# A modulation vector moved to GpSimd, and modulation rows fetched a unit earlier, in a two-layer FoX / GLA trunk

## The chip, the cores and the metric

The kernel runs on one core of a Trainium2 chip. The metric is the device time of one execution in microseconds. The engines are TensorE (PE, with its weight loads PEld), VectorE (DVE), ScalarE (ACT), GpSimd (POOL) and SyncE (SP), which here issues the transfers. Each engine takes its instructions strictly in the order in which they stand in its queue.

## The reference

The trunk has two layers. Layer 0 mixes tokens with forgetting attention (16 heads of 64, 1024 tokens), layer 1 with gated linear attention; each is followed by a SwiGLU channel mixer with 2816 hidden columns. All is fp32.

```python
c_act = jax.nn.silu(c)
for i in range(DEPTH):                       # 2
    mod = c_act @ ada_w[i] + ada_b[i]        # 1024 -> 6 x 1024
    sh1, sc1, g1, sh2, sc2, g2 = jnp.split(mod, 6, axis=-1)
    h = modulate(rms_norm(x, norm1_g[i]), sh1, sc1)
    y = forgetting_attention(h, ...) if i == 0 else gated_linear_attention(h, ...)
    x = x + g1[:, None, :] * y
    h = modulate(rms_norm(x, norm2_g[i]), sh2, sc2)
    x = x + g2[:, None, :] * swiglu(h, ffn_w_in[i], ffn_w_out[i])
return rms_norm(x, final_g)
```

Twelve modulation vectors of 1024 values are needed, numbered here as the kernel does: j = 0 to 5 for layer 0 (sh1, sc1, g1, sh2, sc2, g2) and 6 to 11 for layer 1. Each is a product of one vector with a 1024 x 1024 matrix.

## The kernel before

**Matmuls.** Every fp32 operand is split into a high and a low part (`split`, L175 on ScalarE and L176 on VectorE), and every product is three matmuls (`mm3`, L317 to L319). The channel mixer runs a recursive 2x2 scheme with seven products in place of eight; its sums of weight blocks are made by GpSimd (L951 to L963), its sums of results by VectorE out of the accumulators (L1717), and the derived hidden blocks by GpSimd (L1677 to L1703) and split at L1595 and L1596.

**Modulation vectors.** Vectors 0 and 1 are made at the start, partly on TensorE. The others are made beside the matmuls on VectorE or GpSimd: a row block of `ada_w` is fetched (`ada_load`, L454: four transfers, each to 32 partitions), and then 128x256 blocks of it are multiplied by a column of the activated conditioning vector (`c42`) and added to an accumulator. `ada_steps` does this on VectorE, one fused multiply-add per block (L515 for the first, L517): eight loads with four blocks each where `nt` is 4, or sixteen with two where it is 2. `ada_pool` does it on GpSimd with a multiplication (L478) and an addition (L480) per block, in one buffer that is fetched again after its second block. `ada_end` (L460) closes a vector with two small matmuls with a matrix of ones in quadrants, and VectorE adds the bias (L463).

**Pacing.** These functions are generators, and a `Pace` object advances one of them: each call adds to a balance, and each `yield` takes its value from it. `ada0` holds vectors 2 and 3 (VectorE, in attention), `ada0p` vector 4 (GpSimd, in attention), and `ada1` vectors 5, 6, 7 (in the first channel mixer), 8, 9, 10 (in the second token mixer) and 11 (in the second channel mixer). In the first channel mixer `prod` calls `ada1(0.64 * n)` for each product (n is 4, or 3 or 4 in the second half), and a step takes ADA_A = 4 units between its load and its two blocks and ADA_B = 2 after them. All three vectors are finished (`ada1.flush`) before the last two groups of the first half; vector 5 is the gate of this same mixer.

**Attention.** A unit is a head and a quarter of the queries; there are eight for each pair of heads. `weave` runs the units of pair p against the q and k projections (`qk_proj`) and the v projection (`v_half`) for the next pair. A unit's score matmuls are reduced by VectorE (L1331), exponentiated by ScalarE (L1335), scaled by GpSimd (L1337), transposed by TensorE (L1357), split, and multiplied with v (L1369, L1371); VectorE and ScalarE empty the result (L1386, L1387). The projections' accumulators, two PSUM banks, are emptied in `q_evac` (L867 to L871) and `k_evac`. From the third pair on, each projection ends with `ada0(1.6)`: one or two loads, each followed at once by its four VectorE steps. The raw rows come from a ring of three buffers, `wr`, which the weight loads (`load_w`, L228, split at L243 and L247) use too.

**The order.** The kernel's text gives each instruction a place in the trace order. A planner that simulates the engines then sets the order in each engine's queue: it takes the earliest traced instruction that it holds to be ready, so an instruction may be drawn ahead of others. Where the kernel writes `tc.issue_after`, `in_order`, `behind_one` or a lag in `weave`, the order on that engine is fixed by hand. A step of `ada_steps` with `ahead` is tied behind the VectorE instruction that was traced just before it; those in attention (`ahead` is 0) are not, but for the first, which is tied behind an early instruction.

Of the kernel before, what the change touches and what calls it, by code (L numbers as in the profile page):

```python
# [53 lines left out]
def trunk(ctx, tc, x, c, ada_w, ada_b, norm1_g, norm2_g, ffn_w_in, ffn_w_out,  # L54
# [123 lines left out]
    wr = Ring(big, names[0:3])  # L178
# [75 lines left out]
    split_after = {}  # L254
# [232 lines left out]
    def ada_steps(l, j, acc, raw_of, nt, ahead):  # L487


        steps, got = deque(range(32 // nt)), deque()  # L490

        def load():
            if not steps:
                return
            n = steps.popleft()
            raw = raw_of([P, nt * 256], F32, f"ada{l}{j}{n}").rearrange("p (t c) -> p t c", t=nt)
            ada_load(raw, l, j, n, nt)
            got.append(raw)

        for _ in range(ahead):  # L500
            load()
        for n in range(32 // nt):
            load()
            if ahead:
                yield ADA_A
            raw = got.popleft()
            with ExitStack() as es:
                if ahead:
                    es.enter_context(tc.issue_after(last_of("D")))
                elif n == 0:  # L510
                    es.enter_context(tc.issue_after(split_after["D"]))
                for t in range(nt):
                    o = (0 if nt == 4 else 32) + t * (32 // nt) + n
                    if n == t == 0:
                        nc.vector.tensor_scalar(acc, raw[:, t], c42[:, o:o + 1], None, op0=ALU.mult)  # L515
                    else:
                        nc.vector.scalar_tensor_tensor(acc, raw[:, t], c42[:, o:o + 1], acc,  # L517
                                                       op0=ALU.mult, op1=ALU.add)
            yield ADA_B if ahead else 1.0
        ada_end(l, j, acc)  # L520
        yield 1.0

# [19 lines left out]
            while self.q:  # L542
                self(1.0)

    ada0, ada0p, ada1 = Pace(), Pace(), Pace()

    def ada1_queue(js, acc, raws_):
        r = Cycle(raws_)
        for j in js:
            ada1.q.append(ada_steps(*divmod(j, 6), acc, r, 2, len(raws_) - 1))  # L550
# [736 lines left out]
    def qk_proj(p, i):  # L1287

        if i == 0:
            qkt[p] = qk_tiles(p)  # L1290
        wt = feed.next()
        feed.depth = 3
        for hf in range(2):
            ps = pj([P, HALF], F32, f"qk{i}{p}{hf}")
            yield from proj(ps, wt, hT, hf)
            (k_evac if i else q_evac)(ps, qkt[p], hf)
        if p > 1:
            ada0(1.6)

    oTs = {}  # L1300

# [99 lines left out]
    def attention(p):  # L1401
        for a in range(2):
            h = 2 * p + a
            for i, g in enumerate(ORDER):
# [10 lines left out]
                elif i == 3:  # L1415
                    load_far(h + 1)
                    load_cum(h + 2)
                if p:
                    ada0p(0.8)
                if pending[0] is not None:  # L1420
                    yield from finish(*pending[0])
# [91 lines left out]
    oh = new_h("oh")  # L1513
# [38 lines left out]
    def ffn(l, oh, xs, slots, nm, mid, norm_end, each=None, blocks=None):  # L1552
# [153 lines left out]
        def prod(w, t):  # L1706
            ps = pin([P, HALF], F32, f"p{l}")
            n = len(t)
            for k in range(n):
                mm3(ps, w.hi[:, k, :], w.lo[:, k, :], hi(t[k]), lo(t[k]), k == 0, k == n - 1)  # L1710
            tick()
            ada1(0.64 * n)
            return ps

        def add(G, key, ps, src=None):
# [154 lines left out]
        for X in gs[2:]:  # L1870
            up = lambda n: advance(n) if X is gs[-1] else None
            if X is gs[-2]:
                ada1.flush()
                nxt[0] = part(0)
                advance(4)
            nc.scalar.copy(dest(X, C11), prod(feed.next(), B11))
# [84 lines left out]
        n = 4 if each else 2  # L1961
# [68 lines left out]
    slots = ffn_slots(rest)  # L2030
# [16 lines left out]
            marks["G0"] = last_of("G")  # L2047
        return gates

    def mid(*js):  # L2050
        v = Views(slots["hid"], 2, [HALF], f"ad{js[0]}").v
        ada1_queue(js, v[0][:, 0:256], v[1:4])
        ada1.at -= 20.0

    ADA_A, ADA_B = 4.0, 2.0
    ffn(0, oh, xs, slots, "fo", lambda: mid(5, 6, 7), norm_mixer)
    h1 = hs1
    after_norm = marks.pop("G0")
    split_after.update(marks)
# [557 lines left out]
```

## Time and profile before

| | us |
|---|---|
| Three runs, median (lowest, highest) | 2351.62 (2349.36, 2352.88) |
| The profiled execution, its own time | 2348.59 |
| Its span, first to last instruction | 2346.8 |
| PE busy in the span | 2321.1 (99%) |
| DVE busy | 1786.4 (76%) |
| ACT busy | 1124.0 (48%) |
| POOL busy | 1155.3 (49%) |

A row of the profile names the line of the kernel, the engine, the operation, the tile that it writes and those that it reads, the count, the busy time and the mean duration in ns, then the idle time of the engine just before these instructions and what ended it. `DMA x<-y` as a releaser is the landing of a transfer. Names end in `_s` for SBUF slots and `_b` for PSUM banks: `ad_s` and `acc_s` are modulation accumulators and rows, `ada_s` a row in attention, `mp_b` the bank in which a vector is closed, `o_s` and `xv_s` weights of the mixer, `p_b` its accumulators. In a list of waits, each row gives the engine and tile that waited, on what, and then the total, the count and the longest.

### The profile page before, as it was taken

The page shows a single profiled execution, that of the slowest core. Times are in us where ns is not written, and L with a number is a line of the kernel's source. Part 1 is how long each engine was busy: PE and PEld are TensorE (multiplying, and loading weights), DVE is VectorE, ACT ScalarE, POOL GpSimd, SP SyncE. Part 2 cuts the span into 40 slices and gives each one's busy share as a digit, 9 for nine tenths or more (in the row PEclk, how much of TensorE's full clock was granted, in tenths as well). Part 3 has the DMA queues.
Part 4 walks back from the last instruction along what each step waited for, and adds up shares of the span by engine and source line. Part 5 has one row for each costly group of instructions (what it writes and reads, how often), then busy time and mean ns, then how long its engine had stood idle before and what let it go on. Part 6 is the DMA issues. An engine that isn't in the chain of part 4 may idle for free.

```text
span 2346.8 us, 35574 instructions
## 1 busy us (share of the span) xinstructions
PE 2321.1 (99%) x12088; PEld 1977.9 (84%) x12088; DVE 1786.4 (76%) x2946; ACT 1124.0 (48%) x2166; POOL 1155.3 (49%) x1027
## 2 busy tenths in 40 slices
PE   8999999999999999999999999999999999999999
PEld 7998888888888788788888899898888888888888
DVE  6577777787788998986788666667787777876787
ACT  6566656675543333344325654345444333345236
POOL 1334545543445656564553522345456666664651
PEclk8999999999999999999999999999999999999999
DMA  8533433342425555558774443554434544458774
GB/s 265 159 91 108 120 115 109 112 153 96 153 97 174 188 181 174 163 188 315 252 269 156 135 126 101 152 171 168 149 105 159 178 144 162 139 189 302 236 263 141
DMA packets 359343, 390.72 MB, mean 166 GB/s; under 512 B 26909, under 2 KB 296377, under 8 KB 359161
## 3 DMA queue, kind: packets, MB, share of 16 engines
q1 hardware_dynamic: 359160, 388.45, 50.7%
q8 instruction: 95, 1.56, 0.3%
q14 instruction: 88, 0.71, 0.1%
HBM read 287.10 MB, written 101.25 MB: 165 GB/s over the span
## 4 chain that ended last, share of the span: by engine, by line
PE 53%; DVE 5%; issue 4%; POOL 3%; DMA 2%; ACT 1%; SPq 0%; DVEq 0%; POOLq 0%; ACTq 0%
PE p_b L317 11%; PE p_b L319 11%; PE p_b L318 11%; PE gv_b L319 1%; PE gv_b L317 1%; PE gv_b L318 1%; PE gr_b L317 1%; PE gr_b L319 1%; PE gr_b L318 1%; DVE ad_s L517 1%; DVE o_s L176 1%; PE gqp_b L317 1%; PE gqp_b L319 1%; PE gk_b L317 1%; PE gqp_b L318 1%
## 5 line engine op out<-in xcount | busy, mean ns | idle before, releaser
L175 ACT CAST o_s<-xv_s 128x512 fp32r<-128x512 f32 (+1 forms) x392 | 236.4, 610 | 326.8 <-PE p_b L319 236.7
L176 DVE TENSOR_TENSOR o_s<-xv_s,o_s 128x512 fp32r<-128x512 f32 (+1 forms) x392 | 339.9, 871 | 46.9 <-ACT o_s L175 46.3
L317 PE MATMUL p_b<-B,o_s 128*128 128x512 f32 x608 | 236.1, 391 | 2.7 <-DVE x L1717 1.8
L319 PE MATMUL p_b<-B,o_s 128*128 128x512 f32 x608 | 236.0, 389 | 0.0
L318 PE MATMUL p_b<-B,o_s 128*128 128x512 f32 x608 | 236.0, 389 | 0.0
L951 POOL TENSOR_TENSOR ex_s<-xv_s,xv_s 128x512 f32<-128x512 f32 (+1 forms) x64 | 94.8, 1481 | 251.1 <-DMA xv_s<-in_ffn_w_in_dram 128.0
L1337 POOL TENSOR_SCALAR lp_s<-lp_s,st 128x128 f32<-128x128 f32 (+7 forms) x128 | 97.3, 764 | 224.0 <-DVE st L1336 193.5
L318 PE MATMUL p_b<-T,o_s 128*128 128x512 f32 x480 | 186.7, 389 | 0.0
L317 PE MATMUL p_b<-T,o_s 128*128 128x512 f32 x480 | 186.7, 389 | 0.0
L319 PE MATMUL p_b<-T,o_s 128*128 128x512 f32 x480 | 181.3, 389 | 0.0
L317 PEld LDWEIGHTS p_b<-B,o_s 128*128 128x128 f32 x608 | 114.1, 188 | 28.2 <-DVE x L1717 2.9
L1335 ACT ACTIVATE lp_s<-lp_s,st 128x128 f32<-128x128 f32 (+7 forms) x128 | 99.3, 776 | 76.5 <-DVE st L1331 74.8
L319 PEld LDWEIGHTS p_b<-B,o_s 128*128 128x128 f32 x608 | 114.1, 188 | 23.9
L318 PEld LDWEIGHTS p_b<-B,o_s 128*128 128x128 f32 x608 | 114.2, 188 | 23.3
L953 POOL TENSOR_TENSOR xv_s<-ex_s,xv_s 128x512 f32<-128x512 f32 (+1 forms) x64 | 94.2, 1471 | 56.8 <-DVE o_s L176 53.3
L1717 DVE TENSOR_TENSOR ex_s<-ex_s,p_b 128x512 f32<-128x512 f32 x140 | 94.0, 681 | 31.7 <-PE p_b L319 31.6
L963 POOL TENSOR_TENSOR xv_s<-xv_s,xv_s 128x512 f32<-128x512 f32 x48 | 66.3, 1381 | 97.9 <-issue 56.8
L175 ACT CAST pt_s<-t_b 128x512 fp32r<-128x512 f32 (+1 forms) x160 | 79.3, 548 | 56.8 <-PE t_b L1357 55.4
L318 PEld LDWEIGHTS p_b<-T,o_s 128*128 128x128 f32 x480 | 90.1, 188 | 18.7
L319 PEld LDWEIGHTS p_b<-T,o_s 128*128 128x128 f32 x480 | 90.1, 188 | 18.7
L317 PEld LDWEIGHTS p_b<-T,o_s 128*128 128x128 f32 x480 | 90.1, 188 | 18.6
L176 DVE TENSOR_TENSOR pt_s<-t_b,pt_s 128x512 fp32r<-128x512 f32 (+1 forms) x160 | 96.3, 631 | 11.8 <-ACT pt_s L175 11.3
(1535 smaller groups left out, 7387.8 us busy)
## 6 DMA issues: line engine op xcount, KB each, us to landing
xv_s<-in_ffn_w_in_dram SPq DMA_DIRECT2D x176, 256.0 KB, 3.3
hid_B<-x SPq DMA_DIRECT2D x66, 512.0 KB, 3.0
ad_s<-in_ada_w_dram SPq DMA_DIRECT2D x448, 64.0 KB, 2.4
hid_T<-x SPq DMA_DIRECT2D x44, 512.0 KB, 2.9
xv_s<-in_ffn_w_out_dram SPq DMA_DIRECT2D x88, 256.0 KB, 3.8
T2o<-hid_T SPq DMA_DIRECT2D x22, 512.0 KB, 6.2
T1o<-hid_T SPq DMA_DIRECT2D x22, 512.0 KB, 6.3
B11o<-hid_B SPq DMA_DIRECT2D x22, 512.0 KB, 7.6
```

Of the source, the lines that this page charges most:

```text
L175: nc.scalar.copy(hi, src)
L176: nc.vector.tensor_sub(lo, src, hi.bitcast(F32))
L317: nc.tensor.matmul(ps, ah, bh, start=start, stop=False, skip_group_check=chain)
L318: nc.tensor.matmul(ps, ah, bl, start=False, stop=False, skip_group_check=chain)
L319: nc.tensor.matmul(ps, al, bh, start=False, stop=stop, skip_group_check=chain)
L517: nc.vector.scalar_tensor_tensor(acc, raw[:, t], c42[:, o:o + 1], acc, op0=ALU.mult, op1=ALU.add)
L951: nc.gpsimd.tensor_add(s1, a21, a22)
L953: nc.gpsimd.tensor_sub(a11, s1, a11)
L963: nc.gpsimd.tensor_sub(r[A12], r[A12], r[A11])
L1335: nc.scalar.activation(lp, lp, AF.Exp, bias=mcur, scale=-1.0, accum_out=st[:, qi, 2:3])
L1337: nc.gpsimd.tensor_scalar(lp, lp, st[:, qi, 3:4], 1.0, op0=ALU.mult, op1=ALU.mult)
L1717: nc.vector.tensor_add(d, d if src is None else dest(G, src), ps)
```

## The change

In the first channel mixer, vector 5 is made by `ada_pool` on GpSimd, paced by a new `Pace` called `ada1p` with 0.075 n per product; its accumulator is the second half of the first of the modulation views, its row buffer the fourth. Vectors 6 and 7 stay on VectorE, with two row buffers in place of three (so one load ahead in place of two) and with ADA_A = 6 and ADA_B = 3. In attention, a step of `ada_steps` now yields 0.5 between its load and its four VectorE instructions, and 0.5 after them, in place of 1.0 after both; no more than two other buffers of the ring may be taken in between. The calls `ada0(1.6)` at the end of the projections go, and each unit from the second pair on calls `ada0(0.4)` ahead of the GpSimd vector's `ada0p(0.8)`.

```diff
@@ ada_steps
             load()
             if ahead:
                 yield ADA_A
+            elif split_after:
+                at = wr.n
+                yield 0.5
+                assert wr.n <= at + 2
             raw = got.popleft()
...
-            yield ADA_B if ahead else 1.0
+            yield ADA_B if ahead else 0.5
         ada_end(l, j, acc)
         yield 1.0
...
-    ada0, ada0p, ada1 = Pace(), Pace(), Pace()
+    ada0, ada0p, ada1, ada1p = Pace(), Pace(), Pace(), Pace()
@@ qk_proj
             (k_evac if i else q_evac)(ps, qkt[p], hf)
-        if p > 1:
-            ada0(1.6)
@@ attention
                 if p:
+                    if p > 0:
+                        ada0(0.4)
                     ada0p(0.8)
@@ ffn
             ada1(0.64 * n)
+            ada1p(0.075 * n)
...
             if X is gs[-2]:
                 ada1.flush()
+                ada1p.flush()
@@ around the mixers
-    def mid(*js):
+    def mid(*js, pool=None):
         v = Views(slots["hid"], 2, [HALF], f"ad{js[0]}").v
-        ada1_queue(js, v[0][:, 0:256], v[1:4])
+        if pool is not None:
+            ada1p.q.append(ada_pool(*divmod(pool, 6), v[0][:, 256:512], v[3]))
+        ada1_queue(js, v[0][:, 0:256], v[1:4 if pool is None else 3])
         ada1.at -= 20.0

-    ADA_A, ADA_B = 4.0, 2.0
-    ffn(0, oh, xs, slots, "fo", lambda: mid(5, 6, 7), norm_mixer)
+    ADA_A, ADA_B = 6.0, 3.0
+    ffn(0, oh, xs, slots, "fo", lambda: mid(6, 7, pool=5), norm_mixer)
```

## The prediction

> **What bounds the kernel now.** I read the profile page first: it gives the span and says which engine fills it.
>
> ```profile
> span 2346.8 us, 35574 instructions
> PE 2321.1 (99%) x12088; PEld 1977.9 (84%) x12088; DVE 1786.4 (76%) x2946; ACT 1124.0 (48%) x2166; POOL 1155.3 (49%) x1027
> ...
> L319 PE MATMUL p_b<-T,o_s 128*128 128x512 f32 x480 | 181.3, 389 | 0.0
> ```
>
> TensorE (PE) is busy for 2321.1 of 2346.8 us. What an edit elsewhere can win is therefore time in which PE stands still, and I looked for it with the table of busy time in the two stretches where the edits lie: attention from its second pair of heads to its seventh (160 to 515 us), and the first channel mixer while its modulation vectors are made (707 to 1030 us), with the mixer's stretch after that.
>
> ```profile
> core 0: us, PE busy (x) PEld busy (x) DVE busy (x) ACT busy (x) POOL busy (x), PEclk, DMA share, GB/s
> 160.00:515.00 355.00, 349.19 (x2261) 308.01 (x2261) 260.91 (x685) 224.25 (x478) 178.02 (x256) 1.00 0.39 119
> 707.00:1030.00 323.00, 317.53 (x1398) 260.93 (x1397) 292.45 (x372) 118.52 (x207) 196.57 (x132) 1.00 0.55 177
> 1030.00:1250.00 220.00, 220.00 (x974) 182.21 (x973) 169.97 (x215) 86.00 (x155) 126.03 (x88) 1.00 0.73 253
> ```
>
> The columns are the length, then the busy time of each engine with its instructions. PE idles 355 - 349.2 = 5.8 us in attention, 323 - 317.5 = 5.5 us in the mixer's first stretch, and not at all after 1030 us. VectorE (DVE) is the contrast: 91% busy before 1030 us (292.45 of 323), 77% after (169.97 of 220). Next, the list of waits for PE in both stretches says who ends that idle time.
>
> ```profile
> PE vps_b L317 <- DVE QB L871: 1.6, 1, 1.6
> PE o_b L1371 <- DVE oT_s L1387: 1.3, 4, 0.4
> PE qk_b L317 <- DVE QB L871: 1.3, 2, 0.7
> PE s_b L1323 <- DVE st L1331: 0.8, 3, 0.3
> ...
> PE mp_b L460 <- DVE ad_s L517: 2.8, 2, 1.6
> PE p_b L317 <- DVE x L1717: 1.8, 2, 1.1
> PE p_b L317 <- DVE sg_s L1717: 0.9, 2, 0.7
> ```
>
> The first four rows are attention: about 5 us, all on DVE results. The last three are the mixer: 2.8 us on the closing matmul of a modulation vector (mp_b, L460), which needs the last DVE step of that vector, and 2.7 us on accumulators that DVE has not yet emptied (L1717). So **the ceiling of the whole change is about 11.3 us**, 0.5% of the time: PE cannot be given back more than it idles, but for the overlap of matmuls that comes below.
>
> **The change, part by part: the mixer.** One vector of three leaves DVE for GpSimd (POOL). On DVE a vector is 32 steps of 128x256; on POOL it is 32 multiplications and 31 additions, the form that attention already runs for another vector.
>
> ```profile
> 707.00:1030.00 323.00, 65.86 (x93) 1.00 0.55 177
> L517 DVE SCALAR_TENSOR_TENSOR ad_s<-ad_s,c,ad_s x130: 467/485/1520, 717.2 to 2039.0; 128x256 f32<-128x256 f32 x130
> L480 POOL TENSOR_TENSOR acc_s<-acc_s 128x256 f32<-128x256 f32 x31 | 23.2, 748 | 1.0
> L478 POOL TENSOR_SCALAR acc_s<-acc_s,c 128x256 f32<-128x256 f32 x32 | 17.0, 531 | 12.4 <-DMA acc_s<-in_ada_w_dram 12.4
> L176 DVE TENSOR_TENSOR pt_s<-t_b,pt_s 128x512 fp32r<-128x512 f32 x68 | 44.8, 685 | 5.2 <-ACT pt_s L175 5.0
> L176 DVE TENSOR_TENSOR o_s<-xv_s,o_s 128x512 fp32r<-128x512 f32 x101 | 98.7, 978 | 9.6 <-ACT o_s L175 9.5
> L1596 DVE TENSOR_TENSOR x<-x,x 128x512 fp32r<-128x512 f32 x20 | 26.2, 1316 | 3.3 <-ACT x L1595 2.5
> L1596 DVE TENSOR_TENSOR x<-sg_s,x 128x512 fp32r<-128x512 f32 x20 | 23.5, 1177 | 4.2 <-ACT x L1595 3.6
> ```
>
> Removed from DVE: 65.86 / 93 = 0.708 us a step, times 32 = **22.7 us**. Added to POOL: 32 x 0.531 + 31 x 0.748 = **40.2 us**, spread at 0.3 of a step per product. A product is 12 matmuls, so 34 steps take 113 products; at 317.5 us of PE for 1398 matmuls that is 0.227 us each, 2.73 us a product, some 310 us in all. POOL goes from 196.6 to about 237 us in 323, 61% to 73%.
>
> That POOL time is not free for DVE. The steps of L517 have a median of 0.485 us and reach 1.52; L176 takes 0.685 us in attention, where one input is an accumulator, and 0.978 us here, where both inputs lie in SBUF; L1596, also with both inputs in SBUF, takes 1.316 and 1.177. Over the plain durations (0.485, and 0.685 for the wide ones) the excess is 65.86 - 93 x 0.485 = 20.8, 101 x 0.293 = 29.6, and 20 x 0.631 + 20 x 0.492 = 22.5 us: 72.9 us of DVE waiting beside 196.6 us of POOL work, 0.37 us for each. 40.2 us more of POOL cost DVE 0.37 x 40.2 = **14.9 us**. The net relief is 22.7 - 14.9 = 7.8 us: DVE's idle time rises from 30.6 to 38.4 us, a quarter. This is much less than one vector of three suggests.
>
> The Trainium skill's page SBUF — State Buffer (Who interferes with whom) says that a DVE instruction with two SBUF inputs and a GpSimd instruction that reads SBUF exclude each other, the later one standing still until the other is done. The rows above agree in kind: only the forms with both inputs in SBUF grow.
>
> For PE: there are two DVE vectors left instead of three, so a third of the 2.8 us on mp_b goes with the count (0.9). The remaining two are paced at 6 + 3 units a step instead of 4 + 2, with 2.56 units per product, and a vector's closing matmul is traced 3 units behind its last step instead of 2; I take half of the remaining 1.9 as gone (0.95). POOL's own closing matmul is traced four products, some 11 us, behind its last addition. Of the 2.7 us behind L1717 I take a third, a little above the quarter by which DVE's idle time grows, because pairs of steps also come 3.5 products apart instead of 2.3 (0.9). With the overlap of successive matmuls that each idle gap also destroys (a 0.389 us matmul, the last row of the page above, issues every 0.227, so some 0.16 us a stop, two stops), **3.0 us**. Bounds: 5.5 us, all the idle time; and a loss, priced among the rivals, if POOL's work blocks DVE more than the mean does.
>
> ```profile
> L454 SPq DMA_DIRECT2D ad_s<-in_ada_w_dram x448: 560/587/1945, 675.1 to 2003.3; - x150
> ...
> SPq L454 <- DVE ad_s L517: 30.6, 19, 3.6
> SPq L454 <- POOL acc_s L480: 28.2, 10, 5.6
> ...
> POOL acc_s L478 <- DMA acc_s<-in_ada_w_dram: 12.4, 4, 4.4
> ```
>
> Its transfers stay on SP's queue, 64 for a vector before and after (448 for seven); what changes is whom SP waits for. In the mixer SP waits 30.6 us for DVE to leave a modulation buffer; with one buffer on POOL it waits for POOL, as in attention (28.2 us in 10 waits, 5.6 at most), with weight loads (L933) and spills (L1648) queued behind. PE has no wait for a weight tile in the rows above, and weights are fetched five ahead, five times 2.73 us; a wait of 5.6 us fits, so I cost it at nothing; without that cover it would be 5.6 us each time. POOL may also stand for its own row as in attention, 12.4 us in four waits. Delayed next would be L951 to L963, which feed those weights.
>
> **The change, part by part: attention.** The 16 loads and 64 steps of two vectors stay. They move from the ends of the q and k projections into the units: a load in one, its four steps in a later one, 0.8 of a half per unit.
>
> ```profile
> 172.22 0.69 DVE L871 SCALAR_TENSOR_TENSOR QB<-qk_b,QB 64x512 fp32r<-64x512 f32 x1
> ...
> 199.87 1.01 DVE L517 SCALAR_TENSOR_TENSOR acc_s<-ada_s,c,acc_s 128x256 f32<-128x256 f32 x2 [5.28 <-DMA ada_s<-in_ada_w_dram]
> DVE acc_s L517 <- DMA ada_s<-in_ada_w_dram: 17.7, 7, 5.4
> L517 DVE SCALAR_TENSOR_TENSOR acc_s<-ada_s,c,acc_s 128x256 f32<-128x256 f32 x55 | 33.1, 602 | 18.3 <-DMA ada_s<-in_ada_w_dram 17.7
> ...
> 130.00:160.00 30.00, 4.42 (x7) 1.00 0.34 97
> 408.00:467.00 59.00, 4.49 (x8) 1.00 0.34 108
> 467.00:515.00 48.00, 0.00 (x0) 1.00 0.51 159
> 467.00:515.00 48.00, 46.15 (x273) 38.86 (x272) 38.20 (x101) 34.30 (x70) 19.05 (x26) 1.00 0.51 159
> ```
>
> DVE stood 5.28 us at 199.87 for a row whose load had just been issued, 17.7 us in seven such waits. If every one went, DVE would have that much more room, but PE has it only where a result was late for PE: the short waits on oT_s and st, 2.1 us, and the two on QB, 2.9. I take two thirds of the short ones (1.4) and half of those on QB (1.45), 2.85 us, because two batches of four no longer follow each other at the end of a projection, just where QB is due.
>
> Against that stands the new end. Fifty-six units call the pacer with 0.4, and 18 units of work need 45 calls, that is until the second or third unit of the seventh pair. Before, no step runs after 467 us (the row of zero). Now four to eight steps of 0.602 us do, 2.4 to 4.8 us of DVE, where PE already idles 48 - 46.15 = 1.85 us. The DVE has 9.8 us free there, so most is covered; I put 0.35 us for it, with 4.8 us as the bound if none is covered. **Net 2.5 us**, between a gain of 5.8 us and a loss of 4.8. The rows' loads now stand ahead of the loads of the masks and sums on SP; what would be late next is L1331, which reads them. The weight loads share the ring of three buffers with the rows; a row held a unit longer delays the third load after it, which a projection needs only units later.
>
> **The sum.** 3.0 + 2.5 = 5.5 us. The profiled execution took 2348.59 us, 1.8 beyond its span; it becomes 2343.1. The three runs have their median 3.0 us higher, at 2351.62, so the same step gives **2346.1 us**. A measurement of this kernel tells about 0.2%, 4.7 us, from no change; my forecast lies just beyond that.
>
> **The rivals.**
>
> *The change does not do what it says* (2350.6 us). An order made by a planner need not follow the trace order. The steps at 139 us (the row 130 to 160 us holds seven) are traced behind a q projection whose accumulator DVE empties (L871) at 172 us, so steps are drawn forward until their load seems landed; a load traced a unit ahead may be drawn forward with them, and DVE would still wait. For it: POOL's rows, traced ahead already, still cost POOL 12.4 us. Then attention gives nothing, and the mixer's count alone 0.9: about 1 us.
>
> *POOL shuts DVE out* (2357.6 us, the slower side). A multiplication and an addition run back to back, 1.28 us in which no two-input DVE step proceeds. If the added POOL time costs DVE all of itself, 40.2 - 22.7 = 17.5 us are added to DVE, its idle time falls from 30.6 to 13.1 us, and the 5.5 us of PE idle time grow in proportion of the lost room, by 30.6 / 13.1, to 12.8: 7.3 us more, less 1.3 from attention. It decides from the point where a POOL us costs DVE more than 22.7 / 40.2 = 0.56 us; the rows show 0.37. The rule of the Trainium skill named above (SBUF — State Buffer, Who interferes with whom), taken at its word, gives this case when POOL always starts first; the trace agrees that DVE can stand for a whole POOL instruction (1.52 us at most on L517), though not that it always does.
>
> *Both stages lose nearly all their idle time* (2340.6 us): 11 us, if every stop is the tail of a DVE queue that was only just late. For it: none is longer than 1.6 us. Against: attention's stops recur where no step of L517 is near.
>
> **How the numbers follow.** Forecast 0.50, no effect 0.28, POOL shutting DVE out 0.12, all the idle time 0.10. Of the forecast's own 0.50, a gain of 3 to 8 us, about 0.40 lie beyond 4.7 us; with the last rival, faster has 0.50. The first rival (less 0.02) and the rest of the forecast make 0.36 for no change, and 0.14 is left for slower. The range 2340 to 2354 us reaches from all the idle time to the loss of 4.8 us in attention beside the mixer's gain (2353.4), and leaves out the slow rival and little else.
>
> **What would show it.** In the changed profile: L478 and L480 with 64 and 62 instructions, and 32 fewer on L515 and L517; DVE's share between 707 and 1030 us down by about 8 us only, and two-input durations of L176 and L1596 longer; the wait of mp_b on DVE below 1 us; no wait of L517 for a row longer than 2 us in attention; PE idle at 3 us in each stretch instead of 5.5 and 5.8. Wrong: waits of L517 for ada_s that still sum to more than 10 us; PE waiting for QB or st after 467 us for more than 3 us; any PE wait for a weight tile or for POOL in the mixer.

## The result and the profile after

The changed kernel takes 2361.31 us (median of six runs, 2359.28 to 2362.58), against 2351.19 for the kernel before in the same comparison. The ratio is 1.0043, with a 95% interval of 1.0030 to 1.0056: **slower by about 10 us**, where 5.5 us faster was forecast. The range, 2340 to 2354 us, does not hold it.

The profiled execution took 2361.16 us. From the page of the changed kernel:

```profile
span 2359.4 us, 35610 instructions
PE 2324.2 (99%) x12088; PEld 1975.5 (84%) x12088; DVE 1769.6 (75%) x2914; ACT 1123.0 (48%) x2166; POOL 1207.6 (51%) x1090
```

The table of its busy time in three of the stretches of the prediction (columns as there):

```profile
160.00:515.00 355.00, 349.11 (x2259) 307.98 (x2258) 258.53 (x679) 224.66 (x480) 179.26 (x258) 1.00 0.40 117
707.00:1030.00 323.00, 311.42 (x1347) 252.85 (x1346) 268.59 (x329) 113.53 (x199) 237.21 (x188) 0.99 0.53 171
1030.00:1250.00 220.00, 220.00 (x974) 182.27 (x973) 168.33 (x214) 85.56 (x153) 126.61 (x88) 1.00 0.72 254
```

The count of matmuls in a stretch of fixed length says how far the kernel has come. In attention it is 2259 against 2261: nothing lost, nothing won. Between 707 and 1030 us it is 1347 against 1398. The 51 missing matmuls, at the 0.227 us of the prediction, are 11.6 us of the 12.6 by which the span grew. After 1030 us PE has no idle time, as before. **Nearly the whole loss lies in the first channel mixer, while the vectors are made.**

PE idles 323 - 311.4 = 11.6 us there instead of 5.5, so 6.1 us of the 11.6 lost are more idle time (that the two sums have the same value is chance). Of the other 5.5 us, some 3 lie behind the longest stop, which ends at 869.5 us. The granted clock of PE fell to half there (stretch, length, PE busy with its instructions, granted clock, DMA share, GB/s):

```profile
865.60:869.50 3.90, 0.16 (x1) 0.92 0.77 261
869.50:875.70 6.20, 6.18 (x17) 0.50 0.40 113
```

At a clock of 0.50, 6.2 us do the work of 3.1. The kernel before has no such stretch between 707 and 1030 us, and the prediction has no term for one. The remaining 2.4 us were not traced further.

The waits of PE between 707 and 1030 us (total, count, longest):

```profile
PE p_b L317 <- DVE x L1722: 6.9, 4, 3.8
PE p_b L317 <- DVE sg_s L1722: 3.8, 4, 1.3
PE p_b L317 <- DVE ex_s L1722: 0.3, 1, 0.3
```

L1722 is L1717 of before. The wait on the closing matmul (2.8 us) is gone, as forecast, but the waits for accumulators that VectorE has not yet emptied grew from 2.7 to 11.0 us. The longest wait of GpSimd in the same stretch, with the number of its line unchanged:

```profile
POOL ad_s L478 <- DMA ad_s<-in_ada_w_dram: 21.9, 5, 6.0
```

Here GpSimd stands for its own row. And VectorE in attention, where L521 is L517 of before:

```profile
DVE acc_s L521 <- DMA ada_s<-in_ada_w_dram: 22.6, 7, 5.3
```

It still stands 22.6 us for rows, against 17.7 before, where this was to end.

### The profile page after: what moved, and what is told of

Same layout as the page of the kernel before. It is cut to its first block, busy times and chain, and to the rows that moved or that the text cites. A ratio compares the mean times of both kernels' runs of the same rounds, so it can differ in the third digit from the quotient of the medians.

```text
span 2359.4 us, 35610 instructions
## 1 busy us (share of the span) xinstructions
PE 2324.2 (99%) x12088; PEld 1975.5 (84%) x12088; DVE 1769.6 (75%) x2914; ACT 1123.0 (48%) x2166; POOL 1207.6 (51%) x1090
## 4 chain that ended last, share of the span: by engine, by line
PE 59%; POOL 5%; DVE 5%; DMA 4%; issue 3%; SPq 1%; ACT 1%; DVEq 0%; POOLq 0%; ACTq 0%
PE p_b L317 12%; PE p_b L319 12%; PE p_b L318 12%; DMA ad_s<-in_ada_w_dram 2%; PE gv_b L317 1%; PE gv_b L319 1%; PE gv_b L318 1%; PE gr_b L317 1%; PE gr_b L319 1%; PE gr_b L318 1%; DVE ad_s L521 1%; SPq L454 1%; DVE x L1600 1%; POOL sg_s L1707 1%; DVE o_s L176 1%
## 5 line engine op out<-in xcount | busy, mean ns | idle before, releaser
L176 DVE TENSOR_TENSOR o_s<-xv_s,o_s 128x512 fp32r<-128x512 f32 (+1 forms) x392 | 341.8, 877 | 47.1 <-ACT o_s L175 43.6
L1722 DVE TENSOR_TENSOR ex_s<-ex_s,p_b 128x512 f32<-128x512 f32 x140 | 93.9, 680 | 30.8 <-PE p_b L319 30.6
L247 POOL TENSOR_TENSOR w_l_s<-w__s,w_h_s 128x256 fp32r<-128x256 f32 x90 | 70.5, 812 | 68.1 <-ACT w_h_s L243 68.1
```

Source lines behind the costliest of these rows:

```text
L176: nc.vector.tensor_sub(lo, src, hi.bitcast(F32))
L247: (nc.gpsimd if i < 3 else nc.vector).tensor_sub(lo[:, cs], rw[:, cs], hi[:, cs].bitcast(F32))
L1722: nc.vector.tensor_add(d, d if src is None else dest(G, src), ps)
```

## The experiments

Medians are in us; the kernel before took between 2349.1 and 2350.3 beside them. The ratio is to it.

### Which half of the change

`attention_only` has the mixer of before; `mixer_only` has the attention of before.

```diff
# attention_only
-    ADA_A, ADA_B = 6.0, 3.0
-    ffn(..., lambda: mid(6, 7, pool=5), norm_mixer)
+    ADA_A, ADA_B = 4.0, 2.0
+    ffn(..., lambda: mid(5, 6, 7), norm_mixer)
# mixer_only: ada0(1.6) again at the ends of the projections, no ada0(0.4) in the units, 1.0 after a step
```

> The attention part alone; the first mixer makes vectors 5, 6, 7 on VectorE with 4 + 2 units as before. If the loss lies in the mixer, the time is that of before within 3 us (2348 to 2354), and TensorE idles about 5 us in attention as in both profiles. If the loss lies in attention, it is 2358 or more. The prediction's own price for this part is 2.5 us of gain.

> The mixer part alone; attention as before. If the loss lies in the mixer: 2359 to 2364, with VectorE waiting some 25 to 30 us for ScalarE's casts of the hidden blocks (7 us before) and TensorE idling about 11 us between 707 and 1030 us. If it lies in attention, or only both together make it: within 3 us of before. The prediction's price for this part is 3.0 us of gain.

Measured: attention_only 2349.21, ratio 0.9998 (0.9989 to 1.0007); mixer_only 2360.1, ratio 1.0043 (1.0030 to 1.0056). The attention half does nothing that can be measured, and the mixer half is the whole loss. In attention_only VectorE's wait for rows is there as well:

```profile
DVE acc_s L521 <- DMA ada_s<-in_ada_w_dram: 22.4, 7, 5.3
```

Seven waits, 5.3 us the longest, as before the change. Tracing the load a unit earlier did not part it from its steps: in the changed kernel the step at 197.07 us began to wait at 192.05 us, and the last transfer of its row was issued at 192.3 us. That the planner draws the load and its steps forward together, as the first rival said, fits this, but no run here shows the planner's reason.

### What the sixth vector costs, on GpSimd and at all

`no_vector5` makes only the first product pair of vector 5. `one_row` does all 63 instructions on GpSimd, but on a row fetched once.

```diff
# no_vector5
-        for n in range(16):
+        for n in range(1 if j == 5 else 16):
# no_vector5 and one_row
-                if t and n < 15:
+                if t and n < 15 and j != 5:
```

> The changed kernel with vector 5 left out but for its first row: GpSimd does 2 multiplications and 1 addition for it in place of 32 and 31, and one row is fetched. If GpSimd's work on vector 5 (by its time, its lock, its waits or its place in the queue) is what makes VectorE late, the loss goes, and with a third of VectorE's steps gone the time falls below before: 2343 to 2349. If the other part of the mixer's change (two row buffers in place of three, 6 + 3 units) causes the loss, it stays at 2358 or more.

> The changed kernel with all 63 GpSimd instructions for vector 5, but its row is fetched once and used sixteen times (the vector is wrong in value). If GpSimd is late because it stands still for its own row (21.9 us in five waits), the time returns to 2349 to 2354 and VectorE's waits for the casts fall to about 10 us. If the 40 us of GpSimd work in the queue ahead of the hidden blocks is enough, or the lock that the two engines share is, it stays at 2357 to 2363.

Measured: no_vector5 2342.98, ratio 0.9971 (0.9960 to 0.9982); one_row 2351.82, ratio 1.0007 (0.9998 to 1.0016). So the vector costs 6 us where it was, on VectorE, and 18 us on GpSimd; GpSimd's 63 instructions on one row are 8.8 us of these. With them alone the change would have been no change (1.0007): they take back what the removal gives, and the rest of the loss comes with the rows.

### GpSimd's time, or what its reads do to VectorE

`write_only` is one_row with GpSimd's work on the vector replaced by about as much work that reads nothing: 93 writes of zeros.

```diff
+                    if j == 5 and (n or t):
+                        for _ in range(3):
+                            nc.gpsimd.memset(raw, 0.0)
+                    else: ... the two instructions of before
```

> Leaves out vector 5 but its first product; the row is fetched once and, in place of GpSimd's other 62 instructions on it, GpSimd writes zeros over the buffer three times per step (3 x 0.52 us, so about 48 us in all, as much as its steps take, but without reading anything). The kernel with the steps and one fetch took 2351.82, the one without both 2342.98. If GpSimd's time in line is what costs (what it delivers comes late): 2350 to 2353, with the same TensorE waits for the added blocks of the combining step. If the shutting out of VectorE by GpSimd's reads is what costs: 2343 to 2345, VectorE's lengthening per 1400 products near the 66 us of the kernel without vector 5 and not the 84 us of the one with the steps. Between them, both count.

Measured: 2343.12, ratio 0.9969 (0.9958 to 0.9979), the same as without the vector at all. The stretch of 707 to 1030 us in no_vector5, write_only and one_row, in this order:

```profile
707.00:1030.00 323.00, 323.00 (x1432) 267.51 (x1431) 268.93 (x348) 122.72 (x213) 202.88 (x136) 1.00 0.50 168
```

```profile
707.00:1030.00 323.00, 322.33 (x1425) 265.84 (x1425) 274.18 (x346) 120.24 (x211) 239.56 (x226) 1.00 0.50 167
```

```profile
707.00:1030.00 323.00, 316.47 (x1389) 260.08 (x1388) 279.06 (x340) 118.63 (x206) 245.10 (x191) 0.99 0.49 166
```

The groups of VectorE's remaining modulation steps there, in the same order (busy time, mean ns, then the idle time before them; L525 is L521), and for no_vector5 and one_row the splits of weights:

```profile
L176 DVE TENSOR_TENSOR o_s<-xv_s,o_s 128x512 fp32r<-128x512 f32 x103 | 97.9, 952 | 4.4 <-ACT o_s L175 4.3
L521 DVE SCALAR_TENSOR_TENSOR ad_s<-ad_s,c,ad_s 128x256 f32<-128x256 f32 x32 | 18.7, 583 | 0.2
L521 DVE SCALAR_TENSOR_TENSOR ad_s<-ad_s,c 128x256 f32<-128x256 f32 x30 | 17.7, 589 | 3.8 <-DMA ad_s<-in_ada_w_dram 3.6
```

```profile
L525 DVE SCALAR_TENSOR_TENSOR ad_s<-ad_s,c 128x256 f32<-128x256 f32 x30 | 20.0, 668 | 2.8 <-DMA ad_s<-in_ada_w_dram 2.5
```

```profile
L176 DVE TENSOR_TENSOR o_s<-xv_s,o_s 128x512 fp32r<-128x512 f32 x100 | 100.4, 1008 | 5.5 <-ACT o_s L175 5.4
L521 DVE SCALAR_TENSOR_TENSOR ad_s<-ad_s,c,ad_s 128x256 f32<-128x256 f32 x32 | 21.9, 683 | 0.2
L521 DVE SCALAR_TENSOR_TENSOR ad_s<-ad_s,c 128x256 f32<-128x256 f32 x30 | 27.9, 931 | 2.2 <-DMA ad_s<-in_ada_w_dram 1.9
```

GpSimd's groups for the vector, in write_only and in one_row:

```profile
L480 POOL MEMSET ad_s<- 128x512 f32 x93 | 49.1, 528 | 2.6
```

```profile
L480 POOL TENSOR_TENSOR ad_s<-ad_s,ad_s 128x256 f32<-128x256 f32 x31 | 28.5, 918 | 1.5
L478 POOL TENSOR_SCALAR ad_s<-ad_s,c 128x256 f32<-128x256 f32 x32 | 27.6, 862 | 0.0
```

In write_only GpSimd is busy 239.6 of 323 us, in one_row 245.1, and in no_vector5 202.9. If GpSimd's time in line were short, write_only would lose what one_row loses; it loses next to nothing (1425 matmuls against 1432 and 1389). What differs is that one_row's instructions read SBUF: the larger group of VectorE's steps takes 931 ns there, 668 in write_only and 589 with neither. Sorted by what ran beside them, the splits on VectorE (L176, all with both inputs in SBUF here) take 682 ns on average beside nothing but memsets (19 of them, in write_only) and 684 alone, but 1222 beside GpSimd instructions that read (69 in the same run; in one_row 1197, 81 of them). My theory up to here had been that GpSimd's time runs short, so that the casts, and VectorE behind them, come late; this run ends it.

The Trainium skill, page SBUF — State Buffer (Who interferes with whom), says just this: a VectorE instruction with two SBUF inputs collides with a GpSimd instruction that reads SBUF, and not with one that only writes it. The trace agrees (682 against 1197).

How that becomes a stop of PE is seen ahead of the longest one of the changed kernel, 3.8 us, which ends at 869.5 us. These are VectorE's instructions before it (start, duration, instruction, in brackets its idle time):

```profile
858.76 1.81 DVE L1600 TENSOR_TENSOR x<-sg_s,x 128x512 fp32r<-128x512 f32 x1 [1.70 <-ACT x L1599]
860.49 1.22 DVE L176 TENSOR_TENSOR o_s<-xv_s,o_s 128x512 fp32r<-128x512 f32 x1
861.63 0.67 DVE L1722 TENSOR_TENSOR x<-x,p_b 128x512 f32<-128x512 f32 x1
862.23 1.19 DVE L176 TENSOR_TENSOR o_s<-xv_s,o_s 128x512 fp32r<-128x512 f32 x1
863.34 0.67 DVE L1722 TENSOR_TENSOR x<-x,p_b 128x512 f32<-128x512 f32 x1
863.94 1.18 DVE L1600 TENSOR_TENSOR x<-sg_s,x 128x512 fp32r<-128x512 f32 x1
865.05 1.50 DVE L521 SCALAR_TENSOR_TENSOR ad_s<-ad_s,c 128x256 f32<-128x256 f32 x1
866.47 0.67 DVE L1722 TENSOR_TENSOR x<-x,p_b 128x512 f32<-128x512 f32 x1
867.06 1.18 DVE L176 TENSOR_TENSOR o_s<-xv_s,o_s 128x512 fp32r<-128x512 f32 x1
868.17 0.69 DVE L521 SCALAR_TENSOR_TENSOR ad_s<-ad_s,c 128x256 f32<-128x256 f32 x1
868.79 0.67 DVE L1722 TENSOR_TENSOR x<-x,p_b 128x512 f32<-128x512 f32 x1
```

VectorE had stood 1.7 us for ScalarE before 858.76, and has no gap after it. The add at 868.79 is the one that PE waits for. Ahead of it in the queue stand six instructions with two SBUF inputs that are well above their plain durations: 1.81, 1.22, 1.19, 1.18 and 1.18 instead of 0.685, and 1.50 instead of 0.485 (the two of the prediction), 4.2 us together, against a stop of 3.8. In the same 10 us GpSimd ran two pairs of the vector's instructions, and two additions more, beside the block sums that it always makes there:

```profile
858.03 0.74 POOL L480 TENSOR_TENSOR ad_s<-ad_s,ad_s 128x256 f32<-128x256 f32 x1
858.72 1.29 POOL L1681 TENSOR_TENSOR sg_s<-sg_s,sg_s 128x512 f32<-128x512 f32 x1
859.97 1.19 POOL L480 TENSOR_TENSOR ad_s<-ad_s,ad_s 128x256 f32<-128x256 f32 x1
861.12 1.75 POOL L1686 TENSOR_TENSOR sg_s<-sg_s,sg_s 128x512 f32<-128x512 f32 x1
862.95 1.63 POOL L1690 TENSOR_TENSOR sg_s<-sg_s 128x512 f32<-128x512 f32 x1
864.53 1.73 POOL L967 TENSOR_TENSOR xv_s<-xv_s,xv_s 128x512 f32<-128x512 f32 x1
866.24 0.65 POOL L478 TENSOR_SCALAR ad_s<-ad_s,c 128x256 f32<-128x256 f32 x1
866.97 0.73 POOL L480 TENSOR_TENSOR ad_s<-ad_s,ad_s 128x256 f32<-128x256 f32 x1
867.67 0.92 POOL L478 TENSOR_SCALAR ad_s<-ad_s,c 128x256 f32<-128x256 f32 x1
868.68 0.77 POOL L480 TENSOR_TENSOR ad_s<-ad_s,ad_s 128x256 f32<-128x256 f32 x1
```

GpSimd reads without a break, so VectorE is shut out again and again in a stretch where it has no slack. Two of the six (862.23 and 863.94) ran beside block sums alone, and the kernel before has such sums too. So the list shows how collisions in a row become a stop, not that the vector's instructions make all of it. `mixer_only` has the same instructions of VectorE ahead of the same stop (3.8 us, up to 874.4 us).

### The rest: rows and waits

One_row leaves 9.5 us of the changed kernel's time unexplained, and three runs go after it. `two_rows` fetches each row one step ahead into a second buffer (the complete computation); `spare_row` fetches all rows, 15 of them into a buffer that nobody reads; `narrow_steps` keeps all transfers and waits, with GpSimd's instructions on 32 columns in place of 256. `rows_only` is no_vector5 with the 15 rows fetched for nobody.

```diff
# two_rows: at the start of each step
+            raw = rows_[n % 2]
+            if n < 15: ada_load(rows_[(n + 1) % 2], l, j, n + 1, 2)
# spare_row
-                    ada_load(raw, l, j, n + 1, 2)
+                    ada_load(spare, l, j, n + 1, 2)
# narrow_steps: y, raw[:, t] and acc as [:, 0:32] but for the first
# rows_only: no_vector5, and then
+            for n in range(1, 16):
+                ada_load(spare, l, j, n, 2)
+                yield 2.0
```

> The changed kernel with a second row buffer for vector 5: each row is fetched while the row before is worked on. All of the reference is computed. If GpSimd's standing for its row is what costs the 9 us between one_row (2352) and the changed kernel (2361), its wait (21.9 us) falls below 8 us and the time to 2350 to 2355. If the 64 transfers themselves (on SP's queue and the DMA engines) cost it, the time stays at 2358 to 2363.

> The changed kernel with the later 15 rows of vector 5 fetched into a buffer that nothing reads, while GpSimd uses the first row sixteen times (the vector is wrong in value). The transfers are issued and carried, GpSimd does not wait for them, and SP does not wait for GpSimd. If the waits for the row cost the 9 us: as one_row, 2349 to 2355. If the transfers cost it: 2358 or more.

> The changed kernel with GpSimd's 63 instructions for vector 5 kept, and their waits and transfers, but all after the first on 32 columns of 256 (the vector is wrong in value), so that GpSimd's 40 us shrink to about 12. If the waits for the row alone make the loss, the time stays near 2358 and GpSimd still waits some 20 us for its row. If GpSimd's time in its queue, and the lock that VectorE meets, is the cause, the time falls to 2344 to 2350.

> Leaves out vector 5 but its first row, like the kernel without vector 5 (2342.98 us), but fetches its other 15 rows all the same into a buffer that nothing reads: the transfers and SyncE's issues alone, without GpSimd's work and without anybody who waits. If GpSimd's time is what is missing (working theory): 2343 within 2, no wait of TensorE in the first mixer's products. If the fetches cost by themselves (SyncE late with weights, or the queues): 2348 to 2352, with TensorE waits of 2 us or more in that stretch. If they cost only while GpSimd waits in line behind its own work and delays SyncE, 2343 as well.

| | us | ratio (95%) | matmuls, 707 to 1030 us |
|---|---|---|---|
| no_vector5 | 2342.98 | 0.9971 (0.9960 to 0.9982) | 1432 |
| write_only | 2343.12 | 0.9969 (0.9958 to 0.9979) | 1425 |
| narrow_steps | 2346.81 | 0.9986 (0.9977 to 0.9995) | 1418 |
| rows_only | 2349.17 | 0.9994 (0.9985 to 1.0003) | 1403 |
| one_row | 2351.82 | 1.0007 (0.9998 to 1.0016) | 1389 |
| two_rows | 2354.51 | 1.0017 (1.0008 to 1.0026) | 1378 |
| spare_row | 2359.01 | 1.0038 (1.0025 to 1.0051) | 1361 |
| after | 2361.31 | 1.0043 (1.0030 to 1.0056) | 1347 |

The longer the time, the fewer the matmuls, without exception. Two_rows has everything but GpSimd's wait for its row, 2.7 us above one_row and 6.8 below the change. Narrow_steps has the transfers and the waits but little of GpSimd's work, and loses only 3.8 us against no_vector5, although GpSimd still stands for its row:

```profile
POOL ad_s L479 <- DMA ad_s<-in_ada_w_dram: 16.6, 6, 4.9
```

So a reading is 2343.0 + 8.8 (GpSimd's reads) + 2.7 (the transfers) + 6.8 (GpSimd standing for its row in one buffer, with its full work behind it) = 2361.3. It isn't proof. The terms are differences between orders of the planner, and between medians of different comparisons, in which the kernel before moved by about 1 us; the intervals of one_row and two_rows overlap, so their 2.7 us may be nothing. That the wait alone costs 6.8 us, narrow_steps speaks against. And the clock has a part in the terms: between 707 and 1030 us it stood at 0.50 for 3.4 us in one_row, two_rows and mixer_only, for 6.8 us in the changed kernel, and at no time in the other runs of the table.

Spare_row does not wait either, and stays at 2359.0. It and rows_only fetch in a burst (66 and 67 transfers between 700 and 760 us; two_rows 34, the change 36), and the stops of rows_only, 5.3 us in four, all lie between 738 and 788 us. The burst costs about the same with GpSimd's work (7.2 us, spare_row above one_row) and without it (6.2, rows_only above no_vector5). That it is the burst, and not the rows as such, is argued from two_rows, not shown.

### Other places and another pace

The other runs moved the work elsewhere. `quiet_steps` and `quiet_two_rows` (the latter with the second row buffer) let GpSimd's steps, at twice the rate, only beside products ahead of which no deferred group of block sums is pending (the kernel's list `late` is empty); `quiet_vector` does so with all three vectors on VectorE. `late_vector7` and `late_vector7b` make vector 7 on VectorE in the second half of the mixer instead (7b begins it in the last two groups of the first), vectors 5 and 6 staying on VectorE in the first, at 6 + 3 units.

```diff
# quiet_steps, quiet_two_rows
-            ada1p(0.075 * n)
+            if not late:
+                ada1p(0.15 * n)
# quiet_vector (on the kernel before)
-            ada1(0.64 * n)
+            if l: ada1(0.64 * n)
+            elif not late: ada1(1.28 * n)
# late_vector7, late_vector7b (on the kernel before)
+            ada1l(1.0)                  # in prod; a Pace with vector 7, one row ahead
+            yield 3.2                   # per row; 7b: 2.4, and begun some 40 products earlier
-    ffn(..., lambda: mid(5, 6, 7), norm_mixer)
+    ffn(..., lambda: mid(5, 6), norm_mixer)
```

> The changed kernel, but GpSimd's steps for vector 5 are advanced at twice the rate and only by products during which no derived hidden block is pending. All of the reference is computed. In the changed kernel 18.6 us of these steps lie inside the eight stretches of 6 to 8 us in which GpSimd derives the hidden blocks, and TensorE's stops lie in or just behind these stretches. If the steps there are what makes VectorE late: no step lies in them, the stops between 707 and 1040 us fall from 13.5 to below 5 us, and the time to 2345 to 2351. If transfers, waits for rows or GpSimd's total make the stops: 2357 to 2363 and stops above 10 us.

> As quiet_steps, with a second row buffer for vector 5, so that each row is fetched while the one before is worked on. All of the reference is computed. If the steps' place and the wait for the row both cost: below quiet_steps, 2343 to 2348. If the place is all, as quiet_steps within 2 us; if neither, 2352 to 2357 as two_rows.

> The kernel before, but VectorE's steps for vectors 5, 6 and 7 are advanced at twice the rate and only by products during which no derived hidden block is pending. All of the reference is computed. If TensorE's stops of before (6.4 us in this stretch) come from VectorE's own steps inside those stretches: stops below 3 us and 2345 to 2348. If VectorE is short of time as a whole, the stops move between the stretches: 2349 to 2355.

> The kernel before, with vectors 5 and 6 made in the mixer's first half by VectorE at 6 + 3 units, and vector 7 in its second half, also by VectorE, with the mask tiles as accumulator and row. All of the reference is computed, and GpSimd gets nothing. If VectorE's share in the first half alone sets TensorE's idle time there, as no_vector5 says (nothing idle, 2343), and the second half has room (TensorE never idle from 1030 to 1250 us, VectorE 77% busy): 2343 to 2346. If the second half loses what the first gains: 2348 or more.

> As late_vector7, but vector 7 is made some 40 products earlier: over the last two groups of the first half and the first 28 products of the second, so that its rows are no longer on SP's queue in the stretch from 1150 to 1250 us, where late_vector7 lost 13 us to weights that came late. All of the reference is computed. If those rows held the weights back: TensorE idles nowhere from 707 to 1250 us and the time is 2343 to 2346. If the second half loses it wherever the rows lie: 2350 to 2357.

Measured: 2369.82 (ratio 1.0083, 1.0070 to 1.0096), 2363.41 (1.0063, 1.0051 to 1.0076), 2371.76 (1.0095, 1.0079 to 1.0110), 2355.01 (1.0017, 1.0009 to 1.0026) and 2354.56 (1.0027, 1.0018 to 1.0036). The three quiet runs lie above every range that was expected, the two late ones where they were expected if the second half loses what the first gains. Gathering the same work into less time is worse on either engine. In quiet_steps GpSimd's 63 instructions end at 898 us, in the change at 993; so these runs changed the place and the density together, and don't tell what the place alone is worth. Late_vector7 shows both sides: PE has no idle time between 707 and 1030 us, but between 1030 and 1250 us it gets through 917 matmuls where the kernel before has 974 (the same stretch in the prediction): 57 x 0.227 = 12.9 us lost there, with one stop of 5.4 us and a clock of 0.50 for 6.8 us from its middle on.

`vector5_early` takes vector 5 to VectorE in attention, with the change's pacing; `vector5_early_b` does the same on the kernel before. Both have 6 + 3 units in the mixer.

```diff
-    for j in (2, 3):
+    for j in (2, 3, 5):                 # ada0(0.6) for 0.4; in the second: ada0(2.4) for 1.6
-    ffn(..., lambda: mid(6, 7, pool=5), norm_mixer)
+    ffn(..., lambda: mid(6, 7), norm_mixer)
```

> The complete computation: the changed kernel, but vector 5 is made by VectorE in attention (three vectors there in place of two, drawn 1.5 times as fast), the mixer keeps vectors 6 and 7 on VectorE and none on GpSimd. VectorE has 94 us idle of 355 in attention and 22.7 us are added there; the mixer should lose the 5.5 us of idle it has before. If attention's idle is free: 2343 to 2345, faster than both. If attention's in-order waits take it back (VectorE waits for rows up to 11 us more, TensorE waits there over 5.8 us): 2347 to 2352.

> The complete computation: the kernel before, with vector 5 moved into attention in the same way (2.4 in place of 1.6 units per projection) and 6 and 7 left on VectorE in the mixer at the changed kernel's spacing. Against the run beside it, only the spacing in attention differs. If the spacing has no effect, as with two vectors (0.9998), the two agree within 1.5 us; if the spread over the units matters once attention is fuller, this one is 2 us or more slower.

Measured: 2350.62 (ratio 1.0004, 0.9996 to 1.0013) and 2348.71 (0.9990, 0.9981 to 0.9999). The mixer loses its idle time, as without the vector, and attention takes it back:

```profile
160.00:515.00 355.00, 344.38 (x2219) 303.67 (x2217) 265.46 (x697) 217.09 (x466) 178.61 (x253) 0.99 0.43 127
707.00:1030.00 323.00, 323.00 (x1430) 267.38 (x1429) 270.75 (x349) 124.19 (x214) 199.88 (x135) 1.00 0.52 174
```

```profile
160.00:515.00 355.00, 346.75 (x2233) 304.68 (x2232) 270.43 (x701) 218.78 (x468) 176.58 (x253) 1.00 0.42 128
707.00:1030.00 323.00, 323.00 (x1430) 267.40 (x1429) 268.45 (x350) 123.67 (x214) 200.05 (x134) 1.00 0.51 170
```

PE idles 10.6 and 8.3 us in attention, 5.8 before. The second is the best complete version of the study, 0.1% below the kernel before, which its interval barely tells from no change.

`one_issue` (on the kernel before) and `one_issue_after` fetch a row by one transfer to 128 partitions in place of four.

```diff
-        for q in range(4):
-            nc.sync.dma_start(raw[32 * q:32 * q + 32], src[:, 256 * q:256 * q + 256].rearrange("(r t) c -> r t c", t=nt))
+        nc.sync.dma_start(raw, src.rearrange("(r t) (q c) -> q r t c", t=nt, q=4))
```

> The complete computation: the kernel before, but each row of modulation weights is fetched by one transfer of all 128 partitions in place of four of 32, so SyncE issues a quarter as many (the bytes are the same). Fetching the rows of vector 5 for nobody took the kernel without it from 2343.1 to 2349.2. If what they cost is SyncE's time in line (some 0.585 us an issue, ahead of the weights): most of the 5.5 us of idle that TensorE has before in the first mixer's products goes, 2343 to 2346, and more from the later stages that fetch rows. If it is the bytes, or the queues' time: 2348 to 2351. If one transfer of 64 KB per quarter row in one piece lands later and SyncE's order of waits changes: slower, over 2352.

> The same edit on the changed kernel (2361.3). If the issues are what the rows cost and it adds up with GpSimd's steps (9 us measured with one row): 2352 to 2356. If the bytes or GpSimd's steps hold all of the loss: 2359 to 2362. In both cases it stays above the run beside it by 8 us or more if GpSimd's shutting out of VectorE is the larger part of the change's loss.

Measured: 2475.17 (ratio 1.0521, 1.0507 to 1.0535) and 2495.97 (1.0616, 1.0602 to 1.0631). They don't tell issues from bytes, because the one transfer is itself far slower; its wait in one_issue, and in the kernel before, stands in these rows of VectorE's waits in attention:

```profile
DVE acc_s L515 <- DMA ada_s<-in_ada_w_dram: 53.7, 8, 9.2
```

```profile
DVE acc_s L517 <- DMA ada_s<-in_ada_w_dram: 17.7, 7, 5.4
```

## Why the prediction was wrong

**The step that failed** is "The net relief is 22.7 - 14.9 = 7.8 us": that VectorE's time in the stretch is one account, where the sum decides and 7.8 us to the good make PE's stops shorter. One of its entries was too small, though not so that the sum changes its sign. The vector's 63 instructions on GpSimd took 27.1 + 25.7 = 52.8 us, not 40.2: the prediction priced them as in attention, at 748 and 531 ns. At its own 0.37 that makes 19.5 us for VectorE and leaves a relief of 3.2.

```profile
L480 POOL TENSOR_TENSOR ad_s<-ad_s,ad_s 128x256 f32<-128x256 f32 x31 | 27.1, 874 | 1.4
L478 POOL TENSOR_SCALAR ad_s<-ad_s,c 128x256 f32<-128x256 f32 x32 | 25.7, 805 | 22.1 <-DMA ad_s<-in_ada_w_dram 21.9
```

GpSimd's busy time in the stretch grew by only 40.6 us (237.2 - 196.6), because 50.3 of the 52.8 us lie there and its other work came to 186.9 us instead of 196.6; that 40.6 is near the forecast 40.2 is luck. What the collisions cost by the groups of no_vector5 and one_row: the 62 steps grew from 36.4 to 49.8 us, a hundred splits by 56 ns each, 5.6 us, and the forty of L1600 fell by 2.8 (1302 and 1256 to 1231 and 1185 ns); 16.2 us beside 42.2 us more of GpSimd, 0.38 for each (forecast 0.37). VectorE's account even closed better than forecast: 268.6 us for 1347 matmuls are 278.8 for the 1398 of before, 13.7 us less than 292.5, where 7.8 was forecast. And PE stood still twice as long. By the list ahead of the 3.8 us stop, what decides is how long VectorE is held up at one time, in the few microseconds ahead of an add that PE needs; there a step that VectorE does itself costs 0.485 us, while GpSimd's pair in its place reads for 1.78 (862 and 918 ns in one_row). Write_only shows that the reads are what costs: 8.7 us less without them. That they cost through such bunches is read from this one stop.

**What I costed at nothing** was the second failure. "POOL may also stand for its own row as in attention, 12.4 us in four waits" became 21.9 us in five, and "a wait of 5.6 us fits, so I cost it at nothing" leaned on weights fetched five ahead. PE indeed never waits for a weight tile, but of the 18.3 us between no_vector5 and the change, 9.5 remain when GpSimd's instructions are accounted for, and the second row buffer alone gives 6.8 back. Part of that is the half clock, which the prediction has no term for either. How the wait for a row becomes lost time of PE stays open: with little work behind it, in narrow_steps, the whole loss was 3.8 us.

**The removal** was undersized: 3.0 us forecast for the mixer, while leaving the vector out altogether gives 6.1 (2349.1 - 2343.0 in one comparison: all the 5.5 us of idle time and a little overlap). The pieces on mp_b were right in kind: that wait is gone altogether.

**The rivals.** "The change does not do what it says" was right for attention: the forecast's 2.5 us there are nothing (ratio 0.9998), the sign "waits of L517 for ada_s that still sum to more than 10 us" came (22.6), and no loss came at the end of attention either: its last step starts at 447.9 us (449.5 before), not after 467. "POOL shuts DVE out" named the right mechanism for the mixer and the right side, but its condition, more than 0.56 us of VectorE per us of GpSimd, was not met and was not needed; 2357.6 from a proportion of lost idle room is near 2361.3 by chance. I gave it 0.12 because I let the mean price (0.37) decide, which is the same fault as in the failed step.

**The other signs.** L478 and L480 have 64 and 62 instructions in all, DVE 32 fewer (2914). L176 became longer (978 to 1013 ns); L1600, which is L1596 of before, did not (1316 and 1177 to 1231 and 1186). No PE wait for GpSimd or a weight tile came in the mixer.

## What to carry to other kernels

When work is moved to GpSimd, price its reads where they run beside an engine that is close to late, not by the mean over the stage: a replacement of the same length that reads nothing tells time in line from shutting out in one run. Removing a piece of work altogether, and putting it back in parts (instructions, transfers, waits), shows what each place for it costs before any place is tuned. A load traced earlier helps only if the order that reaches the queue keeps it apart from its users; look at the wait, not at the text.

## What the runs showed of the hardware

GpSimd's memsets cost VectorE's splits nothing, its reads cost them 0.5 us for each that meets one (682, and 1197 to 1222 ns).

A stop of a few microseconds can cost PE more than its own length. After the 3.8 us stop of the changed kernel the granted clock was 0.50 for 6.8 us (868.9 to 875.7 us), and matmuls started every 0.43 us there instead of every 0.227. Behind the same stop in mixer_only it was 0.50 for 3.4 us, likewise behind stops of 2.2 us in one_row and 2.8 us in two_rows, but not behind 2.4 us in spare_row. So these runs give no length from which on it happens.

One transfer of 512 KB to all 128 partitions whose access pattern begins with the four quarters landed 9.1 to 14.0 us after its issue, measured up to the VectorE step that waited for it (ten waits between 150 and 517 us); four transfers of 128 KB each, with 32 partitions first, landed in 2.7 us (median), and their steps waited until 2.8 to 5.6 us after the last issue. The Trainium skill, page DMA: Bandwidth & Descriptors (Why a DMA increments its semaphore by 16 and not by 1), says that a transfer runs on the largest number of DMA engines, at most 16, that divides the slowest dimension of both its patterns: 4 for the one, 16 for the others. The trace agrees in size (about four times as long); it doesn't show the engines of a single transfer.

One vector's rows, 60 transfers of 64 KB, cost time even where no engine reads them: fetched early and for nobody, 6.2 us (2343.0 to 2349.2). Through what, no run here shows.
